# A mixer layer with window attention: projections ahead of their heads, a bounded scale for v, swapped keys by transfer

## The chip, the cores and the metric

The kernel runs on one core of a Trainium2 chip. The metric is the device time of one execution in microseconds. The kernel before took 1007.05 us in the median of three runs (1006.83 to 1008.2).

## What is computed

One layer of a diffusion backbone on 1024 latent tokens (a grid of 16 rows by 64 columns) and 128 context tokens, D = 1024, in float32:

```
h = rmsnorm(x, norm_g) * (1 + scale) + shift            # shift, scale, gate: silu(cond) @ w_ada + b_ada
q, k, v, z_a, u_b, z_b, u_c, z_c, g_a, g_b, g_c = split(h @ w_in)
q, k = rmsnorm(q, q_g), rmsnorm(k, k_g)                 # 8 heads of 64
y_a = softmax over an 8 x 16 window + 128 cached keys   # context tokens: plain attention
y_b = real(fft2(u_b)) @ w_fnet ;  y_c = (window means - u_c) @ w_pool * pool_scale
merged = sum over a, b, c of sigmoid(g) * ((silu(z) * y) @ p)
out = x + gate * (merged @ w_o)                         # also returned: the context tokens' k and v
```

## The kernel before

The tokens are 9 tiles of 128 (tile 8 is the context). Large products are made of three matmuls each (mm3, L143 to L146): both operands are split into a high and a low half of 16 bits (or of rounded float32), and high x high, high x low and low x high are added in PSUM. A weight tile is prepared by a generator (prep, L101): load of the raw weights (L108), sums of squares on ScalarE (L74), a scale that is a power of two (L83 to L91, with a matmul on PE and a power on GpSimd), then the split on ScalarE and VectorE (L98, L99). Raw tiles share NR = 8 slots.

The stages, in order of time: (1) the start, to 69.6 us. The adaLN weights (wa, 16 transfers of 512 KB) and x (9 of 512 KB) are loaded; PE makes the adaLN products (L347) and transposes x (L334) into xT; scale_h (L365) finds a scale for h from a bound. make_h (L385) writes per block k of 128 channels hh and hl, the two halves of h: two ScalarE instructions, two multiply-adds and a subtraction of VectorE (L388 to L391). (2) The early tiles: five token tiles of head pair 0's projection are accumulated beside make_h. (3) The attention stage. A projection of a pair is p1_tiles (L269): per token tile 24 matmuls for q, k and v of two heads, then p1_evac (L214: squares, their sums, a power on GpSimd in rs, v to vraw and its largest value per token) and, half a tile later, p1_norm (L231: four VectorE products into tk, then the halves of q and k into tok, k's high half twice). open_pair (L733) sets a pair up at its first item: pair_setup loads cached keys and values and the bias tables gt; setup_group transposes q and k into q, ka and kb (kb holds the halves of k in swapped order, so that two matmuls give all the products); setup_v finds the largest value of v through PE (pm, pu) and writes v16, and 16 transfers write the windows vw. A pair has 18 items (16 windows of 128 queries, 2 of context), and each goes through five steps one item apart: stage_a scores and bias, stage_b exponential, stage_c transposes, stage_d the product with v, stage_e the transposition of the result py. Between them fill(n) puts n steps (3 matmuls each) of the next pair's projection, 4 an item; beside the last pair those of the u tiles, 6 an item. (4) z and u tiles of branches c and b, the pooling and the Fourier products; (5) P products; (6) za and its P product; (7) the merge gates; (8) the output projection. m_ahead (L191) prepares the weight tile of the next 128 columns in the stages with z and u: load before chunk 0, squares after it, scale after chunk 1, split after chunk 2.

Program order is not the order on the chip. A planner with its own cost model orders the instructions of each engine; it follows the program but moves an instruction ahead when its engine would idle and its operands and buffers are free in the model. It also makes the semaphores. On the chip each engine runs its list in order, and all DMAs stand in one such list, SP's queue. PSUM has eight banks: p1 2, s 2, pt 2, po 1, tr 1.

## Time and profile before

| | |
|---|---|
| median of 3 runs | 1007.05 us |
| the profiled execution, its span | 1008.8 us, 1007.0 us |
| TensorE (PE) busy | 927.9 us (92%) |
| VectorE (DVE), ScalarE (ACT), GpSimd (POOL) busy | 671.1, 523.5, 196.5 us |
| mean granted TensorE clock | 0.977 |

The span is what lies between the first and the last instruction. A busy time is the union of an engine's instructions; matmuls are pipelined, so that two which start 0.16 us apart are shown as 0.33 us long each, and the ends are modelled. A wait is idle time of an engine just before an instruction, with what released it.

### The profile page before, as it was taken

Reading aid. Unit: us, or ns where it says so; the run is one execution under the profiler, and the core shown is the slowest. Engines: PE = TensorE matmul, PEld = TensorE weight load, DVE = VectorE, ACT = ScalarE, POOL = GpSimd, SP = SyncE. Lnnn points to the kernel's source line nnn. Section 1 sums busy time; section 2 is a strip of 40 time slices with the busy share of each in tenths; the row PEclk is TensorE's granted clock in tenths of the full one; section 3 lists DMA queues with packets and bytes.
Section 4 is the critical chain, followed back from the end, with each engine's and each line's share of the span. In section 5 each row is a group of like instructions: output and inputs, shape, how many; then the busy total and the mean of one; then the engine's idle time right before and its main releaser. Section 6 shows DMA issues by size and latency. Waiting matters only on the chain. (4 is left out here: it accounts for less than half of the span.)

```text
span 1007.0 us, 17776 instructions
## 1 busy us (share of the span) xinstructions
PE 927.9 (92%) x6591; PEld 680.3 (68%) x6591; DVE 671.1 (67%) x1568; ACT 523.5 (52%) x1127; POOL 196.5 (20%) x337
## 2 busy tenths in 40 slices
PE   5879897897899899979999899999999999989998
PEld 1325465565666666637897479888888888867886
DVE  1168687677777645696564459878888788766422
ACT  3586766766866856444444534545455444433100
POOL 0114344344344211121200320003021020200000
PEclk9879999999999999979999999999999999999999
DMA  7752223122213322411488502453434332249421
GB/s 274 274 175 80 73 55 72 36 62 66 50 53 63 84 80 82 147 37 53 150 295 301 199 19 95 140 179 98 140 125 152 117 113 92 62 139 307 131 94 53
DMA packets 67415, 121.35 MB, mean 121 GB/s; under 512 B 10064, under 2 KB 34556, under 8 KB 67329
## 3 DMA queue, kind: packets, MB, share of 16 engines
q1 hardware_dynamic: 67329, 120.22, 37.2%
q8 instruction: 52, 0.85, 0.3%
q14 instruction: 34, 0.28, 0.1%
HBM read 87.15 MB, written 28.84 MB: 115 GB/s over the span
## 5 line engine op out<-in xcount | busy, mean ns | idle before, releaser
L144 PE MATMUL p<-wh_q,hh 128*128 128x384 f16 x288 | 96.5, 335 | 1.9 <-ACT hh L388 1.9
L145 PE MATMUL p<-wl_q,hh 128*128 128x384 f16 x288 | 96.2, 334 | 0.0
L146 PE MATMUL p<-wh_q,hl 128*128 128x384 f16 x288 | 94.2, 330 | 0.0
L144 PE MATMUL wo<-woh,mh 128*128 128x512 f32 x144 | 57.1, 396 | 3.6 <-ACT mh L1340 3.6
L146 PE MATMUL wo<-woh,ml 128*128 128x512 f32 x144 | 56.6, 394 | 0.0
L145 PE MATMUL wo<-wol,mh 128*128 128x512 f32 x144 | 56.4, 394 | 0.0
L622 ACT ACTIVATE sn<-sn,mn 128x512 f32<-128x512 f32 x64 | 46.3, 724 | 16.7 <-DVE mn L611 15.7
L635 DVE TENSOR_TENSOR pts<-pt,pts 128x512 f16<-128x512 f32 (+1 forms) x72 | 46.0, 639 | 10.9 <-ACT pts L634 10.9
L611 DVE CUSTOM_DVE_ANT_0 sn<-s,bias 128x512 f32<-128x512 f32 x64 | 43.8, 684 | 12.5 <-PE s L607 12.1
L235 DVE SCALAR_TENSOR_TENSOR tk<-p,rs,grow 128x64 f32<-128x64 f32 x144 | 31.8, 276 | 25.6 <-POOL rs L222 25.6
L1381 DVE TENSOR_TENSOR yo<-wo,gb 128x512 f32<-128x512 f32 x18 | 12.4, 691 | 52.4 <-PE wo L146 52.3
L144 PEld LDWEIGHTS <-wh_m 128*128 128x128 f16 x288 | 29.1, 101 | 24.4 <-ACT wh_m L98 5.8
L145 PEld LDWEIGHTS <-wh_m 128*128 128x128 f16 x288 | 28.8, 100 | 23.5 <-issue 7.5
L88 POOL TENSOR_SCALAR wsc_g<-wsc_g 128x1 f32<-128x1 f32 x12 | 2.8, 231 | 209.0 <-DVE wsc_g L87 209.0
L651 PEld LDWEIGHTS <-pts 128*128 128x128 f16 x792 | 34.9, 99 | 12.2 <-DVE pts L635 6.5
L146 PEld LDWEIGHTS <-wl_m 128*128 128x128 f16 x288 | 28.5, 99 | 20.9 <-issue 1.7
L144 PEld LDWEIGHTS <-hh 128*128 128x128 f16 x288 | 29.0, 101 | 19.4 <-ACT hh L388 2.0
L146 PEld LDWEIGHTS <-hl 128*128 128x128 f16 x288 | 28.7, 100 | 18.7 <-issue 1.4
L634 ACT CAST pts<-pt 128x512 f16<-128x512 f32 (+1 forms) x72 | 38.9, 541 | 3.5 <-PE po L651 1.6
L632 PE MATMUL pt<-ident,sn 128*128 128x128 f32 x256 | 40.0, 277 | 0.8 <-ACT q L506 0.7
L651 PE MATMUL po<-vw,pts 128*128 128x64 f16 x576 | 33.9, 195 | 7.4 <-DVE pts L635 4.3
L145 PEld LDWEIGHTS <-hh 128*128 128x128 f16 x288 | 28.8, 100 | 17.4 <-issue 1.5
(650 smaller groups left out, 3087.6 us busy)
## 6 DMA issues: line engine op xcount, KB each, us to landing
wa<-in_wss_dram SPq DMA_DIRECT2D x16, 512.0 KB
wr_q<-in_w_dram SPq DMA_DIRECT2D x16, 384.0 KB
wr_m<-in_w_dram SPq DMA_DIRECT2D x24, 256.0 KB
pp_c<-pec SPq DMA_DIRECT2D x24, 192.0 KB
pp_b<-peb SPq DMA_DIRECT2D x24, 192.0 KB
pp_a<-pea SPq DMA_DIRECT2D x24, 192.0 KB
ppxc<-pp_c SPq DMA_DIRECT2D x16, 288.0 KB
ppxb<-pp_b SPq DMA_DIRECT2D x16, 288.0 KB
```

The costliest lines, as they stand in the source:

```text
L88: G.tensor_scalar(sc_[:, 2:3], sc_[:, 2:3], 1e-36, None, op0=ALU.max)
L144: T.matmul(out, lh, rh, start=first, stop=False)
L145: T.matmul(out, lh, rl, start=False, stop=False)
L146: T.matmul(out, ll, rh, start=False, stop=last)
L235: ins = V.scalar_tensor_tensor(tkv[:, g], pt[:, g * 64:g * 64 + 64], rs[:, g:g + 1], toks["g"][:, g], op0=ALU.mult, op1=ALU.mult)
L611: V.tensor_tensor_reduce(out=sn, in0=pS, in1=bt.rearrange("p a b -> p (a b)"), op0=ALU.add, op1=ALU.min, scale=1.0, scalar=3e38, accum_out=mn)
L622: S.activation(e[:, :n], it["sn"], AF.Exp, bias=it["mn"], scale=-1.0, accum_out=sm_)
L632: T.transpose(pt[:, j * P:(j + 1) * P], it["e"][:, j * P:(j + 1) * P], ident)
L634: S.copy(pts[:, 0, :n], pt[:, :n])
L635: V.tensor_tensor(pts[:, 1, :n], pt[:, :n], pts[:, 0, :n], op=ALU.subtract)
L651: T.matmul(po[:, :64], it["pts"][:, a, j * P:(j + 1) * P], it["vl"][j][:, c_ * 64:(c_ + 1) * 64], start=(j == 0 and i == 0), stop=(j == nk ...
L1381: V.tensor_tensor(yo, pt, gb[0 if t == 8 else 1][:, cols], op=ALU.mult)
```

## The change

The projection of a pair becomes part of one generator (chain) that also issues the set-up of the pairs at given steps; it starts 41 steps ahead of the first item, gains on the items until item 15, and then keeps its distance. The tiles that two pairs now use at a time have twice the buffers. v is scaled by a bound (from the bound of h, the weights' scale and the largest cached value), so that p1_evac writes its halves straight from PSUM. kb is written by transfers that swap the halves of ka. h is kept in float32 in xT before its scale is known, and make_h then takes one instruction on each of two engines. x and wa are loaded in another order and with more buffers. Weights of z and u are loaded two tiles ahead, and their squares, scale and split come one chunk earlier. The tr bank becomes a second po bank. Cut to its core:

```diff
-NR = 8
-NWA = 4
+NR = 6
+NWA = 6
...
-    BANKS = {"p1": 2, "s": 2, "pt": 2, "po": 1, "tr": 1}
+    BANKS = {"p1": 2, "s": 2, "pt": 2, "po": 2}
...
+        def m_load(i):
+            if i < len(MORDER):
+                munits[i] = prep_m(MORDER[i], f"m{i}")
+                run(munits[i], 1)
         def m_ahead(i, c):
-            if i + 1 < len(MORDER) and i + 1 not in munits:
-                munits[i + 1] = prep_m(MORDER[i + 1], f"m{i + 1}")
-            if i + 1 < len(MORDER):
-                n = {-1: 1, 0: 1, 1: 1, 2: 9}[c]
-                r = run(munits[i + 1], n)
-                if c == 2:
+            if c == -1 and i + 2 < 9:
+                m_load(i + 2)
+            if c == -1 and i == 8:
+                m_load(10)
+            if c == -1 and i > 8:
+                m_load(i + 2)
+            if i + 1 < len(MORDER) and c < 2 and not (c == -1 and i == 8):
+                g = munits[i + 1]
+                n = {-1: 1, 0: 1, 1: 9}[c] + (i == 8 and c == 0)
+                r = run(g, n)
...
+            def new_pair(p, wu):
+                inv = wu["inv"]
...
+                f = qkv.tile([P, 4], F32, tag="vf", name=f"vf{p}", bufs=3)
+                i8, sv, un, scv = (f[:, i:i + 1] for i in range(4))
+                G.tensor_scalar(i8, inv, 0.125, None, op0=ALU.mult)
+                V.tensor_tensor(sv, vrec[:, p:p + 1], inv, op=ALU.mult)
+                V.tensor_tensor(sv, sv, svb, op=ALU.min)
+                pow2(sv)
+                V.reciprocal(un, sv)
+                V.tensor_tensor(un, un, inv, op=ALU.mult)
+                V.reciprocal(scv, un)
+                v16 = qkv.tile([P, 9, 2, 2, 64], F16, tag="v16", name=f"v16{p}", bufs=2)
...
+                rg = qkv.tile([P, 4, 64], F32, tag="rg", name=f"rg{p}_{t}", bufs=2)
+                G.tensor_tensor(rg, c["g"], rs.unsqueeze(2).to_broadcast([P, 4, 64]), op=ALU.mult)
+                pv = pt[:, 256:384].rearrange("p (h d) -> p h d", h=2)
+                S.activation(c["v"][:, t, :, 0, :], pv, AF.Copy, scale=c["sv"])
+                V.scalar_tensor_tensor(c["v"][:, t, :, 1, :], pv, c["sv"], c["v"][:, t, :, 0, :], op0=ALU.mult, op1=ALU.subtract)
...
-                for g in range(4):
-                    ins = V.scalar_tensor_tensor(tkv[:, g], pt[:, g * 64:g * 64 + 64], rs[:, g:g + 1], toks["g"][:, g],
-                                                 op0=ALU.mult, op1=ALU.mult)
-                    tc.keep_in_program_order(ins)
+                V.tensor_tensor(tk, pt[:, :256], rg.rearrange("p g d -> p (g d)"), op=ALU.mult)
...
-                S.copy(qv[:, :, 0], tkv[:, 0:2])
-                S.copy(kv[:, :, 0], tkv[:, 2:4])
-                V.tensor_tensor(qv[:, :, 1], tkv[:, 0:2], qv[:, :, 0], op=ALU.subtract)
-                V.tensor_tensor(kv[:, :, 1], tkv[:, 2:4], kv[:, :, 0], op=ALU.subtract)
-                S.copy(kv[:, :, 2], kv[:, :, 0])
-                toks[t] = t16
...
+                t16 = qkv.tile([P, 4, 2, 64], F16, tag="tok", name=f"tok{p}_{t}", bufs=9)
+                S.copy(t16[:, :, 0], tkv)
+                V.tensor_tensor(t16[:, :, 1], tkv, t16[:, :, 0], op=ALU.subtract)
+                c["toks"][t] = t16
...
+                XG = ((0, 1, 2), (3, 4, 5), (6, 7, 8))
...
+                    V.reciprocal(shs, hm[:, 0:1])
+                    pow2(shs)
...
+                def h_full(k, eng):
+                    for a, c in ((slice(0, NS), 1), (slice(NS, NT), 0)):
+                        if eng is S:
+                            S.activation(xT[:, k, a], xT[:, k, a], AF.Identity, bias=sh[:, k, c:c + 1], scale=gs[:, k, c:c + 1])
+                        else:
+                            V.tensor_scalar(xT[:, k, a], xT[:, k, a], gs[:, k, c:c + 1], sh[:, k, c:c + 1], op0=ALU.mult, op1=ALU.add)
                 def make_h(k):
-                    h32 = st.tile([P, NT], F32, tag="xt", name=f"h32_{k}", bufs=5)
-                    for a, c in ((slice(0, NS), 1), (slice(NS, NT), 0)):
-                        S.activation(hk(hh, k, a), xT[:, k, a], AF.Identity, bias=sh[:, k, c:c + 1], scale=gs[:, k, c:c + 1])
-                        V.tensor_scalar(h32[:, a], xT[:, k, a], gs[:, k, c:c + 1], sh[:, k, c:c + 1], op0=ALU.mult, op1=ALU.add)
                     a = slice(0, NT)
-                    V.tensor_tensor(hk(hl, k, a), h32, hk(hh, k, a), op=ALU.subtract)
+                    S.activation(hk(hh, k, a), xT[:, k], AF.Copy, scale=shs)
+                    V.scalar_tensor_tensor(hk(hl, k, a), xT[:, k], shs, hk(hh, k, a), op0=ALU.mult, op1=ALU.subtract)
...
+                for what in (0, 1, 2, "w0", "w1", 3, 4, 5, "w2", "w3", "w4", "w5"):
+                    load_x(what) if isinstance(what, int) else load_wa(int(what[1:]))
+                nwa = 6
...
+                    if i == 1:
+                        xnorms(XG[0])
+                        run(xg, 8)
+                        for t in XG[2]:
+                            load_x(t)
+                    while nwa < 16 and nwa - 6 <= i:
+                        load_wa(nwa)
+                        nwa += 1
...
+                    if i == 9:
                         run(prep0, 1)
                     if i % 4 == 3:
                         ada_end(i // 4)
+                    if i == 11:
+                        for k in range(6):
+                            h_full(k, (S, V)[k % 2])
                     if i == 13:
+                        run(prep0, 1)
...
+                    if k == 1:
+                        h_full(6, V)
+                    if k == 2:
+                        h_full(7, S)
...
+                    if k == 3:
+                        v_bound(hm)
+                        head_scales(kall)
+                        v_scales(vall)
+                        c0 = new_pair(0, wu)
...
+                def load_bias(c, hd):
+                    p = c["p"]
+                    g = at.tile([P, 1008], F32, tag="gt", name=f"gt{p}_{hd}", bufs=3)
+                    src = bass.AP(tensor=rpbp.tensor, offset=(2 * p + hd) * 23 * 63,
+                                  ap=[[63, 8], [1, 16], [1, 993]])
+                    nc.sync.dma_start(g[:, :993], src)
+                    c["gt"][hd] = g
...
+                def pair_loads(c):
+                    p = c["p"]
                     kr = at.tile([P, 2, P], F32, tag="kr", name=f"kr{p}", bufs=1)
                     nc.sync.dma_start(kr, kctx[p])
                     vr = at.tile([P, 3, 2, 64], F32, tag="vr", name=f"vr{p}", bufs=1)
                     nc.sync.dma_start(vr, vctx[p].rearrange("p (r h d) -> p r h d", r=3, h=2))
-                    gt = []
+                    ka = at.tile([P, 2, 1280], F16, tag="ka", name=f"ka{p}", bufs=2)
+                    kb = at.tile([P, 2, 1280], F16, tag="kb", name=f"kb{p}", bufs=2)
+                    c.update(kr=kr, vr=vr, ka=ka, kb=kb, q=[], bias={}, yt={}, vw=[], gt={})
+                    load_bias(c, 0)
...
+                def swapped(dst, src):
+                    nc.sync.dma_start(dst[0:64], src[64:P])
+                    nc.sync.dma_start(dst[64:P], src[0:64])
...
+                    S.copy(part(c["ka"]), pk if g == 0 else pk.rearrange("p h (a c) -> p h a c", a=2))
+                    for o in ((0,), (512, 1024))[g]:
+                        b = slice(o, o + (512, 256)[g])
+                        swapped(c["kb"][:, :, b], c["ka"][:, :, b])
...
-                    m1 = at.tile([P, 2], F32, tag="m1", name=f"m1{p}", bufs=1)
-                    V.tensor_reduce(m1, vt["mx"].rearrange("p t h -> p h t"), axis=AX.X, op=ALU.max)
-                    pm = bank("tr", f"pm{p}")
-                    T.transpose(pm[:2, :P], m1, ident)
-                    m2 = at.tile([2, 1], F32, tag="m2", name=f"m2{p}", bufs=1)
-                    V.tensor_reduce(m2, pm[:2, :P], axis=AX.X, op=ALU.max)
-                    V.tensor_scalar(m2, m2, 1e-30, 1.0 / 8192, op0=ALU.max, op1=ALU.mult)
-                    dg = at.tile([2, 2], F32, tag="dg", name=f"dg{p}", bufs=1)
-                    V.tensor_scalar(dg, ident[:2, :2], m2, None, op0=ALU.mult)
-                    pu = bank("tr", f"pu{p}")
-                    T.matmul(pu[:, :2], ones8[:2], dg, start=True, stop=True)
...
+                    zb = at.tile([P, 2, P], F16, tag="pqb", name=f"pqb{p}", bufs=2)
+                    swapped(zb, z[:, 2:4])
...
+                def chain():
+                    for p in range(5):
...
+                        elif p < 4:
+                            wu = nextw["wu"]
+                            c = pairs[p] = new_pair(p, wu)
+                            at_(10, pair_loads, c)
+                            at_(14, setup_prompt, c)
+                            at_(18, next_load)
+                            at_(24, pair_cached, c)
+                            for n in (36, 42, 48, 53, 58, 63):
+                                at_(n, next_step)
+                            at_(46, group_q, c, 0)
+                            at_(50, group_k, c, 0)
+                            if p == 3:
+                                at_(66, m_load, 1)
+                            gen = p1_tiles(c, (8, 0, 1, 2, 3, 4, 5, 6, 7), wu)
...
+                        if p > 0:
+                            b = pairs[p - 1]
+                            at_(2, windows, b)
+                            at_(5, group_q, b, 1)
+                            at_(7, group_k, b, 1)
+                        for n, _ in enumerate(gen):
+                            for f, a in ev.get(n, ()):
+                                f(*a)
+                            yield
...
+                fill(32 + 9)
+                LEAD = 16
+                done, want = 9.0, 9.0
                 for j in range(-2, len(items) + 2):
-                    q = 6 if j >= 3 * NI - 2 else 4
-                    if j + 2 < len(items):
-                        it = items[j + 2]
-                        if (j + 2) % NI == 0:
-                            open_pair(it["p"])
-                        if (j + 2) % NI == 1 and it["p"] > 0:
-                            setup_group(cur["c"], it["p"], 1)
-                        if (j + 2) % NI == 12 and it["p"] < 3:
-                            cur["npq"] = setup_prompt(cur["ntk"], it["p"] + 1)
-                        it["c"] = cur["c"]
+                    it = j + 2
+                    want += (72 - 9) / (LEAD - 1) if it < LEAD - 1 else (312 - 72) / (len(items) + 4 - LEAD + 1)
+                    q = int(want - done + 1e-6)
+                    done += q
...
+                    if m == 7:
+                        m_load(9)
...
```

## Rows read from the trace of the kernel before

**Rows 1.** The page: its first line, PE's busy time, and GB/s in 40 slices of 25.2 us
```profile
span 1007.0 us, 17776 instructions
...
PE 927.9 (92%) x6591; PEld 680.3 (68%) x6591; DVE 671.1 (67%) x1568; ACT 523.5 (52%) x1127; POOL 196.5 (20%) x337
...
GB/s 274 274 175 80 73 55 72 36 62 66 50 53 63 84 80 82 147 37 53 150 295 301 199 19 95 140 179 98 140 125 152 117 113 92 62 139 307 131 94 53
```

**Rows 2.** Stretches: length, busy us per engine (instructions), granted PE clock, DMA share, GB/s
```profile
240.00:260.00 20.00, 14.83 (x135) 10.63 (x135) 14.55 (x44) 12.60 (x38) 7.30 (x14) 0.91 0.21 54
...
420.00:440.00 20.00, 14.19 (x78) 8.64 (x76) 19.36 (x31) 8.85 (x17) 6.54 (x5) 0.89 0.11 33
440.00:460.00 20.00, 18.00 (x100) 11.60 (x99) 16.89 (x38) 9.82 (x22) 5.03 (x7) 0.86 0.22 67
460.00:1007.00 547.00, 530.91 (x3531) 432.62 (x3528) 369.95 (x653) 227.20 (x410) 56.65 (x67) 0.99 0.42 140
```

**Rows 3.** PE's waits over the span: waiting line, releaser, us in total, times, longest
```profile
PE py L662 <- DVE yt L653: 10.6, 3, 5.4
...
PE zb L144 <- ACT wh_m L98: 5.4, 1, 5.4
...
PE po L651 <- DVE pts L635: 4.3, 6, 1.0
PE pk L512 <- DVE pts L635: 3.7, 3, 1.2
...
PE pu L545 <- DVE dg L543: 2.8, 3, 0.9
PE po L651 <- DVE yt L653: 2.8, 3, 1.2
PE pq L504 <- DVE tok L248: 2.7, 3, 2.0
...
PE pqp L527 <- DVE tok L248: 2.4, 1, 2.4
```

**Rows 4.** ACT's timeline, 236 to 246 us: start, duration, instruction, idle before, releaser
```profile
241.51 0.63 ACT L74 ACTIVATE wjk_m<-wr_m 128x512 bf16<-128x512 f32 x1 [5.12 <-DMA wr_m<-in_w_dram]
```

**Rows 5.** PE's timeline, 59 to 93 us: start, duration, instruction, idle before
```profile
59.17 1.88 PE L347 MATMUL pa<-wa,sil 128*2 128x512 f32 x4
...
69.60 0.50 PE L144 MATMUL p<-wh_q,hh 128*128 128x384 f16 x1 [1.94 <-ACT hh L388]
...
92.54 0.33 PE L144 MATMUL p<-wh_q,hh 128*128 128x384 f16 x1
92.70 0.33 PE L145 MATMUL p<-wl_q,hh 128*128 128x384 f16 x1
...
93.02 0.22 PE L504 MATMUL pq<-id,tok 128*128 128x128 f16 x1
```

**Rows 6.** Stretches of the start, columns as in rows 2
```profile
8.00:20.00 12.00, 9.28 (x16) 1.50 (x16) 1.53 (x6) 5.69 (x11) 1.29 (x2) 1.00 1.02 406
24.00:30.00 6.00, 6.00 (x29) 2.55 (x27) 0.00 (x0) 2.64 (x5) 0.00 (x0) 1.00 0.48 146
```

**Rows 7.** Waits of SP's DMA queue over the span, columns as in rows 3
```profile
SPq L478 <- POOL bias L585: 74.6, 5, 23.3
...
SPq L294 <- PE pa L347: 18.6, 9, 4.4
```

**Rows 8.** Groups by form, 69 to 430 us: count, busy us, mean ns, idle before
```profile
L235 DVE SCALAR_TENSOR_TENSOR tk<-p,rs,grow 128x64 f32<-128x64 f32 x144 | 31.8, 276 | 25.6 <-POOL rs L222 25.6
...
L584 POOL TENSOR_TENSOR bias<-mk,gt 128x256 f32<-128x256 bf16 x24 | 17.0, 710 | 0.1
...
L391 DVE TENSOR_TENSOR hl<-h,hh 128x1152 f16<-128x1152 f32 x8 | 11.1, 1402 | 0.1
...
L512 PE MATMUL pk<-id,tok 128*128 128x128 f16 x128 | 10.2, 220 | 4.9 <-DVE pts L635 3.7 <-DVE tk L235 0.8 <-DVE tok L249 0.3
```

**Rows 9.** POOL's timeline, 156 to 157 us, columns as in rows 4
```profile
156.04 1.22 POOL L584 TENSOR_TENSOR bias<-mk,gt 128x256 f32<-128x256 bf16 x1
```

More of the change, by code (lines that the diff above doesn't have):

```diff
@@ L713, in start_gen @@
[L713 to L724 removed]
+                pairs = [c0, None, None, None]
```

391 lines of the change are left out of this document (174 added, 217 removed).

## The prediction

> **What bounds the kernel now.** I read the page first [rows 1]: TensorE (PE) is busy for 927.9 of 1007.0 us, more than any other engine, so time can be won where PE waits or works slowly, and by taking PE work away. Next the table of stretches [rows 2]: from 460 us to the end PE is busy for 530.9 of 547 us at a granted clock of 0.99. That stretch holds the pool and Fourier branches' end, the P products, the merge gates and the output projection, and almost nothing is left there to win. Before 460 us it is otherwise: 14.8 of 20 us busy at a pair boundary (240 to 260), 14.2 of 20 where the zc and zb tiles meet (420 to 440). The list of PE's waits [rows 3] names the losers: the transpose py behind yt (10.6 us in 3 waits), zb behind its weights (5.4 us in one), and six smaller ones, of which pk, pu, pq and pqp are the set-up of a head pair. What is behind py is seen on ScalarE (ACT) [rows 4]: it stood 5.12 us at 241.51 on the squares of a weight tile (wjk_m) whose transfer had not landed; these squares are needed only much later, but everything of the attention that ACT has to do stood behind them, and so did VectorE (DVE) and PE. The granted clock of that stretch is 0.91 [rows 2]: PE came back from the wait at the lower of its two levels (1.2 instead of 2.4 GHz). Last, the start: the first projection matmul (p) runs at 69.60 us [rows 5], and until then PE only has the adaLN products and the transposes of x.
>
> **The change part by part.** The sum is made against the profiled execution: 1008.8 us, of which 1007.0 is the span; the median of the runs shown is 1007.05, 1.75 lower.
>
> *The start (loads of x and wa).* Six wa and six xt buffers instead of four and five; x comes in groups of three; the 1.57 MB of the first pair's weights are issued behind all of wa. What must land before the scale of h is known is 9 x and 16 wa transfers of 512 KB, 13.1 MB. The first slice of the page (25.2 us at 274 GB/s) brought 6.9 MB of that [rows 1]. With the engines full the rate is 406 GB/s; from 24 to 30 us it was 146 [rows 6], because the queue stood: it waited 18.6 us in 9 pieces for PE to free wa buffers [rows 7]. If the new order keeps the engines full, the remaining 6.3 MB (with the small tables) take 15.5 us, and the last wa is there at 40.7. From the last adaLN product to the first p matmul it took 69.60 - 59.17 = 10.4 us [rows 5]; the new chain to the scale has as many steps (one more maximum, no multiplication of gs and sh). So the first p matmul comes at 51.1 at the earliest. The weights land 3.9 us behind wa and need some 5 us, which is no later. The buffers still make the queue wait for PE now and then, so I add 4 us and take 55: **-14.5 us**. The bounds are 51.1 (-18.5) and, if the queue stands as before and the weights come behind it, 73.5 (+3.9).
> The Trainium skill (DMA: Bandwidth & Descriptors, Specifications) gives a limit of about 358 GB/s per core from HBM. The 406 GB/s of the row is over it, so the measurement decides; by the page the 6.3 MB would take 17.6 us and the start would be 2.1 us later.
>
> *The early tiles (h in float32, then scaled).* Per block of h, DVE did two forms of multiply-add and a subtraction; now one instruction of 128x1152 (the subtraction took 1.40 us [rows 8]) does it once the scale is known, and the multiply-adds come before it for six blocks. Into this stretch move head_scales, v_scales, v_bound and new_pair, some 30 short DVE instructions with round trips to PE. Before, the stretch from the first p to the first pq took 93.02 - 69.60 = 23.4 us [rows 5], and 120 matmuls at the step of 0.16 us (92.54 to 92.70 [rows 5]) are 19.5. DVE will have about 8 x 1.40 for h, 4 splits and the short ones: as long as PE. I take **+2 us** (0 to +4).
>
> *The attention stage.* The projection of a pair now ends some three items before its heads begin, and its set-up (group_q, group_k, prompt, windows) is spread over the filler steps. What goes: setup_v with its round trip to PE (pu, 2.8), the waits of pq (2.7) and pqp (2.4) for a fresh tok, and pk behind pts (3.7), since half of the pk transposes go and the rest use the po banks: 11.6 us [rows 3]. Their cover is the lead: three items have at least 3 x 12 filler matmuls of 0.16 us, 5.9 us, where a wait for tok was 2.4 at most. What is late next is py: the squares of later weights may still be put ahead of the attention's work on ACT, with six raw buffers instead of eight, but the transfers are written further ahead of them and the bias tables, for which the queue stood 74.6 us [rows 7], get a third buffer. I take half of py's 10.6, 5.3, and one of the two clock losses behind them (0.09 x 20 us, 1.8 [rows 2]). The two po waits (4.3 and 2.8) get a second bank for po, shared with pk, py and the scales: 2. The 64 pk transposes that go are 10.2 us / 2 = 5.1 at most [rows 8]. Together **-25.8 us**; the bounds are -5.1 (every wait comes back under another name) and -38 (all the rows named here, both clock losses).
> Off PE's path, so at nothing: four tk instructions per tile become one, 31.8 us of DVE [rows 8] for 36 x 0.47 (between 0.276 for 64 columns and 1.40 for 1152); maxima of v become a subtraction; three copies on ACT become one; POOL gets one product of 128x256 per tile, 36 x 0.71 = 25.6 us [rows 8], between rs and tk. Its cover is the second p1 bank: a tile needs 24 x 0.16 = 3.9 us of PE even without attention beside it. Without that cover 0.71 us per tile, 26 us, would show.
> The swapped keys are 8 transfers a pair on SP's queue, of 64 partitions each. The trace has none like it; they are between nothing and the 5.12 us that ACT waited for a transfer behind a busy queue [rows 4]. Group 1's are asked for three items before the first item that reads them, 5.9 us of filler alone, so I take nothing; uncovered, 8 groups of them cost 41 us.
>
> *The weights two tiles ahead.* Squares, scale and split of the next weights each come one chunk of 24 matmuls earlier, 3.9 us. zb waited 5.4 [rows 3], so 1.5 remain. The clock of the two stretches around it was 0.89 and 0.86 [rows 2], 0.25 x 20 = 5.0 us; with so short a wait I take 4.0 of it back: **-7.9 us** (0 to -10.4). DVE is full there (19.4 of 20 us [rows 2]), which is the doubt. The rest of the kernel: 0.
>
> The sum: 1008.8 - 14.5 + 2 - 25.8 - 7.9 = 962.6; less 1.75 for the median, **961 us**.
>
> **The rivals.**
> 1. *The waits in the attention stage change their names.* PE's filler and attention come from in-order queues, and DVE stays at three quarters [rows 2]; if a tk behind the longer POOL chain holds up sn or pts, only the removed transposes count. Against it: the waits named stand at set-ups that no longer exist. 961 + 20.7 = 982.
> The Trainium skill (SBUF — State Buffer, Who interferes with whom) says that a DVE instruction with two SBUF inputs and a GpSimd instruction that reads SBUF exclude each other. The trace agrees where it can be seen: at 156.04 POOL's product took 1.22 us [rows 9], its mean is 0.71 [rows 8]; the new product on POOL is of the same form, and stands where such subtractions of DVE are common.
> 2. *The start does not move*, because the transposes of x and the adaLN products free the buffers no sooner than now [rows 7]: 961 + 14.5 = 975.5.
> 3. *All of it goes*: -18.5, 0, -38 and -10.4 give 942.
> 4. *The squares stand more often behind a late transfer: slower.* SP's queue is one queue in order. It now also carries 32 swap transfers, each waiting for an ACT copy, and the raw weight tiles have six slots, so a load stands behind a split of the tile before. Each time ACT meets such squares too soon, PE loses 5.1 us [rows 4] and 1.8 of clock, 6.9 together. It happened three times, twice for long [rows 3]. The change's 46 us are gone from 7 more such stalls; by the code 40 raw tiles are loaded, so there is room for 9: 961 + 62 = 1023. Against it: a load now comes a whole tile ahead of its squares, and the longest waits of the queue, those for the bias tables, have an extra buffer.
> That the change does not do what it says could be so in one respect: the order of instructions is made by a planner that already moves loads and squares far ahead, so "ahead" in the code may be no more than it did before. That is inside rivals 1 and 2.
>
> **How the numbers follow.** Forecast (950 to 969) 0.45; rival 1 and its halves (970 to 990) 0.20; rival 2 0.13; rival 3 0.13; rival 4 0.06; something between, no difference, 0.03. The range 940 to 990 takes in the bounds of the start and of the attention stage and leaves out rival 4 and the far ends. What a measurement of this kernel can tell from no change is 0.2%, 2 us: faster 0.91, within it 0.03, slower 0.06.
>
> **What would show it.** Start: first p matmul near 55 us, DMA near 406 GB/s without the gap at 24 to 30. Attention: pu gone, pq, pk and pqp gone from PE's waits, py at half. Middle: zb's wait under 2 us and a granted clock of 1.00 around it. From there to the end no difference. The forecast is wrong if the first p matmul comes after 65 us, if s waits for the swapped half of the keys, or if ACT's waits for wr transfers become longer or more than in the trace of before.

## The result

The changed kernel takes 996.95 us (median of four runs, 995.81 to 999.48), the kernel before, run beside it, 1007.62 us: a ratio of 0.988 [0.983, 0.993]. It is faster, but by some 11 us and not by the 46 of the forecast, and 997 lies outside the range. The profiled execution is the slowest of the four, 999.48 us; PE is busy for 11.7 us less than in [rows 1], at a granted clock of 0.979:

```profile
span 997.7 us, 17549 instructions
...
PE 916.2 (92%) x6510; PEld 675.4 (68%) x6510; DVE 648.5 (65%) x1431; ACT 495.0 (50%) x1023; POOL 228.5 (23%) x373
```

The landmarks on PE's timeline, of the kernel after (columns as in [rows 5]), cut it into the stages of the sum:

```profile
62.94 0.84 PE L144 MATMUL p<-wh_q,hh 128*128 128x384 f16 x2
...
88.85 0.22 PE L572 MATMUL pq<-id,tok 128*128 128x128 f16 x1
...
94.92 0.29 PE L572 MATMUL pq<-id,tok 128*128 128x128 f16 x1 [5.85 <-DVE tok L279]
...
130.13 0.31 PE L649 MATMUL s<-pqz 128*128 128x128 f16 x1
...
397.58 0.33 PE L144 MATMUL zc<-hh,wh_m 128*128 128x384 f16 x1
...
472.65 0.39 PE L144 MATMUL ppc<-th,oh_pc 128*128 128x384 f32 x1
...
533.02 0.33 PE L144 MATMUL za<-hh,wh_m 128*128 128x384 f16 x1
```

Before, the first p and pq stood at 69.60 and 93.02 [rows 5], and zc, ppc and za at these times:

```profile
401.74 0.33 PE L144 MATMUL zc<-hh,wh_m 128*128 128x384 f16 x1
...
485.30 0.39 PE L144 MATMUL ppc<-th,oh_pc 128*128 128x384 f32 x1
...
542.57 0.33 PE L144 MATMUL za<-hh,wh_m 128*128 128x384 f16 x1
```

| stage, us | before | after | moved | forecast |
|---|---|---|---|---|
| start, to the first p | 69.60 | 62.94 | -6.7 | -14.5 |
| early tiles, to the first pq | 23.4 | 25.9 | +2.5 | +2 |
| attention, to the first zc | 308.7 | 308.7 | 0.0 | -25.8 |
| middle, to the first ppc | 83.6 | 75.1 | -8.5 | -7.9 |
| P products, to the first za | 57.3 | 60.4 | +3.1 | 0 |
| the rest | 464.4 | 464.7 | +0.3 | 0 |

Of the miss of 36.9 us (999.5 for 962.6), 25.8 lie in the attention stage, which gave nothing; 7.8 lie in the start and 3.1 in the P products. PE's waits over the span show what is gone and what came (those of before are [rows 3]):

```profile
PE pq L572 <- DVE tok L279: 19.5, 8, 5.9
...
PE po L702 <- DVE pts L686: 7.5, 10, 1.9
...
PE zb L146 <- DVE wl_m L99: 1.9, 2, 1.4
...
PE py L713 <- DVE yt L704: 1.2, 2, 0.7
```

py fell from 10.6 to 1.2 us, more than half; pu is gone, pk behind pts too (1.8 us stand there behind another releaser), and pqp went from 2.4 to 2.0. But pq, which was to go, rose from 2.7 to 19.5 us, and po behind pts from 4.3 to 7.5. Ahead of both stands a VectorE instruction, tk: tok is made from it, and pts comes later in VectorE's list. Here are VectorE's wait at it over the span of the kernel after, and the groups by form from 60 to 420 us (the tk row of before is in [rows 8], with 25.6 us of waiting):

```profile
DVE tk L271 <- POOL rg L257: 52.6, 34, 3.5
```
```profile
L271 DVE TENSOR_TENSOR tk<-p,rg 128x256 f32<-128x256 f32 x36 | 15.3, 424 | 52.6 <-POOL rg L257 52.6
...
L257 POOL TENSOR_TENSOR rg<-grow,rs 128x256 f32<-128x256 f32 x36 | 22.1, 614 | 2.8
```

tk's own work fell from 31.8 to 15.3 us, near the 16.9 reckoned; its wait doubled.

Two parts of the attention stage moved in opposite directions. The *opening*, from the first pq to the first score matmul s, grew from 21.5 to 41.3 us. About 4 us of this is work that the lead moved into it (108 p matmuls for 84, at a step of 0.16 us). For the rest PE loses both time and clock: it is idle for 16.0 us instead of 4.4, at a granted clock of 0.80 instead of 1.00. The *body*, from the first po to the end of the last py, shrank from 280.2 to 258.9, by 15.2 us of PE's busy time and 6.1 of its idle time. The stretches of the opening, first before, then after, columns as in [rows 2]:

```profile
93.02:114.55 21.53, 17.17 (x123) 9.74 (x121) 15.97 (x55) 16.70 (x42) 12.73 (x21) 1.00 0.27 85
```
```profile
88.85:130.13 41.28, 25.31 (x148) 15.04 (x146) 21.30 (x65) 19.61 (x41) 21.48 (x36) 0.80 0.34 89
```

### The profile page after: what moved, and what is told of

Same layout as the page of the kernel before. It is cut to its first block, busy times and chain, and to the rows that moved or that the text cites. A ratio compares the mean times of both kernels' runs of the same rounds, so it can differ in the third digit from the quotient of the medians.

```text
span 997.7 us, 17549 instructions
## 1 busy us (share of the span) xinstructions
PE 916.2 (92%) x6510; PEld 675.4 (68%) x6510; DVE 648.5 (65%) x1431; ACT 495.0 (50%) x1023; POOL 228.5 (23%) x373
## 4 chain that ended last, share of the span: by engine, by line
PE 65%; DVE 11%; DMA 8%; POOL 7%; ACT 5%; issue 3%; SPq 1%; ACTq 0%; DVEq 0%; POOLq 0%
PE wo L144 3%; PE wo L145 3%; PE wo L146 3%; PE xc L146 3%; PE xb L144 3%; PE xb L146 3%; PE xb L145 3%; PE xc L144 3%; PE xc L145 3%; POOL rs L255 3%; PE xa L144 3%; PE xa L146 3%; PE xa L145 3%; PE ppa L144 2%; PE ppa L146 2%
## 5 line engine op out<-in xcount | busy, mean ns | idle before, releaser
L271 DVE TENSOR_TENSOR tk<-p,rg 128x256 f32<-128x256 f32 x36 | 15.3, 424 | 52.6 <-POOL rg L257 52.6
L145 PEld LDWEIGHTS <-hh 128*128 128x128 f16 x288 | 29.0, 101 | 17.8 <-issue 1.9
L362 PE MATMUL pa<-wa,sil 128*2 128x512 f32 x64 | 31.0, 633 | 10.1 <-DMA wa<-in_wss_dram 10.1
```

Of the source, the lines that this page charges most:

```text
L145: T.matmul(out, lh, rl, start=False, stop=False)
L271: V.tensor_tensor(tk, pt[:, :256], rg.rearrange("p g d -> p (g d)"), op=ALU.mult)
L362: T.matmul(pa[:2], sil[:, k], wa[i][:, q], start=(k == 0), stop=(k == KT - 1))
```

## The experiments

All are edits of the kernel after; ratios are to the kernel before, run beside them. The theory at first was that the opening waits for its set-up; the rivals were the new GpSimd product rg with VectorE's place for tk, and the queues of DMAs.

**The start.** One kernel issues the first wa transfer ahead of x and holds the squares of x behind the condition's exponential; another leaves out half of PE's adaLN products.

```diff
-S.activation(sq, xt[t], AF.Square, scale=1.0 / 32, ...)
+S.activation(sq, xt[t], AF.Square, scale=c32, ...)
...
+c32 = st.tile([P, 1], F32, name="c32")
+V.tensor_scalar(c32, ex[:, 0:1], 0.0, 1.0 / 32, op0=ALU.mult, op1=ALU.add)
...
-for what in (0, 1, 2, "w0", "w1", 3, 4, 5, "w2", ...):
+for what in ("w0", 0, 1, 2, "w1", "w2", 3, 4, 5, ...):
```


> The changed kernel with the first adaLN weight tile loaded ahead of x, and the exponential of the condition tied ahead of ScalarE's squares of x; nothing else. Theory A (PE bounds the start): from the first adaLN product (12.89 us) to the last (54.1) PE has 41.7 us of work and stands for 1.6, so the start moves by as much as the first product moves: it comes at about 9.3, the first projection matmul at 59 to 60 in place of 62.9, and the time is 993 to 995 us. Rival B (the transfers bound it, as the prediction had it): the bytes are the same, so the first projection matmul stays within 1 us of 62.9 and the time within 1 us of 997.


```diff
-for q in range(2):
+for q in range(1):
...
```


> The changed kernel with every second adaLN product left out (32 of 64 matmuls of 2 x 512; all transfers stay), so the shift and scale are of half of the condition. Theory A (PE bounds the start): 15.5 us of PE's 41.7 go; the start shortens until the transfers bound it, so the last adaLN product comes at 40 to 45 us in place of 54.1, the first projection matmul at 49 to 54, and the transfers run near 400 GB/s to the end of wa. Rival B (the transfers bound it already): the last adaLN product comes no earlier than 52 us.

With wa first the first adaLN product ran at 8.54 instead of 12.89 us, but the last ended only 1.5 us sooner and the first p came at 61.43 (from 62.94); s gained 0.5. The whole: 998.66 us, ratio 0.988 [0.985, 0.991], no different from the kernel after. With half the adaLN work (one run, 1000.3 us) the last product still ended at 52.94 (from 54.10), the first p came later, at 65.62, and SP's queue waited longer for PE, 23.2 us; the two rows are of the kernel after and of the one with half the products:

```profile
SPq L308 <- PE pa L362: 17.9, 8, 5.9
```
```profile
SPq L308 <- PE pa L362: 23.2, 8, 9.7
```

So PE's amount of work alone does not set the end. With half of it PE stood 6.3 us at the transposes of x behind VectorE's xt and 3.0 us at pb behind ScalarE's ar, and the granted clock in the three stretches of 10 us from 20 to 50 us was 0.77, 0.89 and 0.83, where the kernel after had 1.00. In PE's list adaLN products stand behind transposes of x, those behind the norms, and those behind x; that this order is the cause was not tested by itself.

**The opening, by its waits.** Four kernels change the place of the set-up: group_q, group_k and the prompt later in the chain; the scales of the cached keys held behind a tile; the same with the bias tables; the squares of the next weights held behind tile 2.

```diff
-at_(4, group_q, c, 0); at_(6, group_k, c, 0); at_(14, setup_prompt, c)
+at_(20, group_q, c, 0); at_(22, group_k, c, 0); at_(24, setup_prompt, c)
```


> The changed kernel with the transposes of pair 0's q and k (group_q, group_k, setup_prompt) at steps 20, 22 and 24 of its chain in place of 4, 6 and 14; nothing else. Theory A (PE's order): the eight transposes stand in PE's queue ahead of projection matmuls whose operands have long been there, so PE stands 6.0 and 2.3 us behind tok and comes back at the lower clock; then these waits go, the granted clock between 80 and 100 us rises from 0.82 to above 0.95, the first transpose of probabilities comes about 10 us earlier, and the kernel takes 986 to 990 us where the changed one takes 997. Rival B (the chain of each tile): the tokens come no faster than the chain squares, sum, power, product, tk, tok through four engines lets them, some 3 to 4 us a tile, so the wait moves to the last tile's transposes near 120 us and the time stays within 2 us of 997.


```diff
+V.scalar_tensor_tensor(tz[:, 0:2], c["rs4"][:, 0:2], 0.0, ksp, op0=ALU.mult, op1=ALU.add)
...
-f = ks_[:, 2 * p + hd:2 * p + hd + 1]
+f = ksp[:, hd:hd + 1]
```


> The changed kernel with the cached keys and values of pair 0 (kh, vc) tied to the fifth early tile by a product with zero, so that ScalarE can't reach them before the first squares of the projection. Theory A: ScalarE stood 5.15 us on the transfer of kr ahead of the first squares (sq at 82.78 us), and all of the opening stands behind that; then sq comes some 4 us earlier, the first wait of pq falls from 6.0 to about 2 us, and the kernel takes 991 to 994 us. Rival B: the first tile's squares also need PE's last matmul of that tile and the scale from VectorE (79.3 us), and GpSimd's long product stands until 77 us; then it is at most 1.5 us earlier and the time is within 2 us of 997.


```diff
...
+if p == 0:
+    for r_ in ((0,) if rb == 0 else (0, 12)):
+        G.tensor_copy(b[:, r_, 0:4], c["rs4"])
```


> The changed kernel with two kinds of work held back until the fifth early tile of pair 0 has its scale (by a product with zero or a copy that is overwritten): the cached keys and values (kh, vc) on ScalarE, and the bias tiles of pair 0 on GpSimd. Nothing else. Moving the wait of PE (groups_late) brought the first scores only 2 us earlier, holding back kh alone 1.2 us. Theory B (the chain of each tile): GpSimd is the narrow place of it, and stands 1.1 us on the transfer of gt with 5 us of bias work among the powers of the first four tiles; then the tokens of tiles 0 to 3 come at 91 to 92 us in place of 97.2, the first scores at 124 to 126 in place of 130.1, and the kernel takes 991 to 993 us where the changed one takes 997. Rival C (the late tiles): the last tiles 5, 6 and 7 wait for banks and for transfers of weights near 115 to 122 us anyway; then the first scores come no earlier than 128.5 and the time is within 2 us of 997.


```diff
-S.activation(jk[:, :n], r, AF.Square, scale=1.0 / 16384, ...)
+S.activation(jk[:, :n], r, AF.Square, scale=sc16, ...)
...
```


> The changed kernel with the squares of the weights of pairs 2 and 3 and of the first u weights tied to the third tile of the pair before (one copy and one small product a pair), so that ScalarE cannot come to them before their transfers are in. Theory C: ScalarE stands 0.84 and 1.42 us on a transfer of wr_q at 117 and 121 us, with the squares of the last early tile behind it; then that tile's token comes 2 to 4 us earlier than 125.7, the first scores at 126 to 128 in place of 130.1, and the kernel takes 993 to 995 us. Rival B: the tile's token is late by its own chain, the first scores move by less than 1 us and the time by less than 1.5.

None opened it. With the groups later the two pq waits before 98 us (7.9 us) were gone, and 7.1 us stood instead at pk and at p behind tk: s gained 2.0, 995.13 us (0.985 [0.982, 0.988]). The others gained 1.2, 1.0 and 1.5 us at s, and the last two, which tie work of later pairs too, lost about 5 us in the body: 997.81 (0.988 [0.985, 0.991]), 1004.6 (0.995 [0.993, 0.998]) and 1000.79 us (0.991 [0.988, 0.994]). The theory of the set-up fell.

**The chain on GpSimd.** One kernel takes the power and rg of pair 0 off GpSimd (its power is left out); one moves rg of all pairs to VectorE.

```diff
-G.tensor_scalar(rs, ss, EPS, None, op0=ALU.add)
-G.tensor_tensor(rs, rs, mhalf, op=ALU.pow)
+if p == 0: V.tensor_scalar(rs, ss, EPS, None, op0=ALU.add)
+else: ...
-G.tensor_tensor(rg, c["g"], ...)
+(V if p == 0 else G).tensor_tensor(rg, c["g"], ...)
```


> The changed kernel with GpSimd taken out of the normalization of pair 0: the sum with epsilon and the product rg on VectorE, and the power (-0.5) left out, so that q and k of the first two heads are scaled wrongly. Pairs 1 to 3 are as in the changed kernel. Theory B (the chain of each tile through GpSimd sets the pace of the opening): 1.9 us of GpSimd and two rounds between engines go from each of nine tiles; pq's waits near 89 to 97 us fall from 8.3 to under 4 us, the token of the last tile of pair 0 comes at 112 to 116 us in place of 126.2, and the first scores at 117 to 121 in place of 130.1. Rival C (the late tiles wait for their projection, banks and transfers): the first scores come no earlier than 126 us.


```diff
-G.tensor_tensor(rg, c["g"], rs.unsqueeze(2).to_broadcast([P, 4, 64]), op=ALU.mult)
+V.tensor_tensor(rg, c["g"], rs.unsqueeze(2).to_broadcast([P, 4, 64]), op=ALU.mult)
```


> The changed kernel with the product rg (128 x 256, one a tile, 36) on VectorE in place of GpSimd. The prediction costed it at nothing, with the second p1 bank as its cover. Theory B (GpSimd's chain sets the pace of the opening): 0.61 us and a round between two engines go from each of nine tiles; the first scores come 3 to 5 us earlier, pq waits less for tok in each pair, and the kernel takes 992 to 994 us. Rival: the second bank covers it as predicted; the first scores move by less than 1 us, VectorE has 36 x 0.4 us more, and the time is within 1.5 us of 997.

Without the chain the opening is 26.9 us long instead of 41.3, with the same 108 p matmuls: PE is idle in it for 5.5 us instead of 16.0, at a granted clock of 0.96. The first bias sum sn stood at 126.25 instead of 139.24, the time of the one run was 988.53 us. The stretch of the opening without the chain (columns as in [rows 2]), and PE's waits from 60 to 137 us, first of the kernel after, then without the chain:

```profile
89.76:116.66 26.90, 21.44 (x149) 13.27 (x147) 21.63 (x74) 18.69 (x41) 6.51 (x14) 0.96 0.47 125
```
```profile
PE pq L572 <- DVE tok L279: 15.1, 4, 5.9
```
```profile
PE pq L575 <- DVE tok L282: 4.7, 3, 4.3
```

What the chain is for one tile is seen in the timelines of POOL, VectorE and ScalarE of the kernel after; the last step of GpSimd is what VectorE waits for, and ScalarE behind it:

```profile
88.69 0.24 POOL L254 TENSOR_SCALAR rs<-ss 128x4 f32<-128x4 f32 x1
89.39 1.03 POOL L255 TENSOR_TENSOR rs<-rs,mhalf 128x4 f32<-128x4 f32 x1
90.50 0.61 POOL L257 TENSOR_TENSOR rg<-grow,rs 128x256 f32<-128x256 f32 x1
```
```profile
91.14 0.42 DVE L271 TENSOR_TENSOR tk<-p,rg 128x256 f32<-128x256 f32 x1 [3.48 <-POOL rg L257]
```
```profile
91.60 0.41 ACT L278 CAST tok<-tk 128x256 f16<-128x256 f32 x1 [3.11 <-DVE tk L271]
```

On VectorE rg brought s 4.6 us sooner, but the body lost 9.8: 1003.84 us (nine of ten runs, 1000.94 to 1007.19; 0.995 [0.993, 0.997]). VectorE's one queue carries the attention too, which is the likely reason.

**What stands behind the waiting tk.** One kernel calls p1_norm three steps later, and the group set-ups with it; one makes the high halves on GpSimd instead of ScalarE.

```diff
-if k == 3 and late:
+if k == 6 and late:
...
-at_(5, group_q, b, 1); at_(7, group_k, b, 1)
+at_(8, group_q, b, 1); at_(10, group_k, b, 1)
```


> The changed kernel with a tile's normalization (tk, tok) issued at step 6 of the next tile in place of step 3 (and group_q, group_k of the second half at steps 8 and 10 in place of 5 and 7, since they read it). Theory R (the first rival of the prediction): between 137 and 397 us VectorE stands 36.4 us in 25 waits at tk for GpSimd's rg, and ScalarE 31.9 us at tok behind it, with the softmax of the heads queued behind both; asked for three steps (9 matmuls, 1.5 us, and the attention between them) later, these waits fall by a third or more, PE's waits for pts fall from 7.5 to below 5 us, and the kernel takes 991 to 994 us. Rival: the order on the engines is made by the planner, which moves tk and tok ahead again, and a bank is held longer; waits and time stay as they are, within 1.5 us of 997.


```diff
-S.copy(t16[:, :, 0], tkv)
+G.tensor_copy(t16[:, :, 0], tkv)
```


> The changed kernel with the first half of the token (tok, the copy of tk, 36 of 128 x 256) on GpSimd in place of ScalarE. Theory R: ScalarE's in-order queue stands 31.9 us in 26 waits at tok for tk, with exponentials and pts behind it; without it ScalarE is free for pts, PE's waits po behind pts (7.5 us) fall by half and the stretch from the first po to the last py is 3 to 6 us shorter than 258.9. Rival: VectorE waits in ScalarE's place (its second half of tok then waits for GpSimd, 0.6 us later), and the stretch is as long or longer.

Three steps later: 994.68 us (0.985 [0.982, 0.988]), some 3 us by the ratios, whose intervals overlap; s came 4.5 us sooner. On GpSimd: 1011.44 us, no faster than the kernel before (1.002 [1.000, 1.004]), with a body of 271.9 us; ScalarE then waited 55 us at sn behind mn, where it had waited 29.

**The two edits at tk, one by one.** Two things were done to tk at once: one product with rg from GpSimd took the place of four that read rs, and the line that kept the four in program order went. The first kernel puts the order back; the second puts the four products back, without the order; the third both; the fourth keeps the order and adds later norms (with the group set-ups) and slots of their own for the P weights.

```diff
-V.tensor_tensor(tk, pt[:, :256], ...)
+tc.keep_in_program_order(V.tensor_tensor(tk, pt[:, :256], ...))
```


> The changed kernel with tk kept in program order among VectorE's instructions, nothing else; the product rg stays on GpSimd and the issue at step 3. It splits what the old normalization gave (972.95 us in place of 997). Theory R1 (the place in the order): VectorE's waits at tk fall from 36.4 to below 25 us, the stretch from the first po to the last py from 258.9 to 250 or less, and the kernel takes 986 to 992 us. Theory R2 (GpSimd's extra step): program order at step 3 is too early for the chain through rg; the waits stay above 30 us and the time within 3 us of 997. In both the opening stays at 40 us or more from the first pq to the first scores.


```diff
-G.tensor_tensor(rg, c["g"], rs.unsqueeze(2).to_broadcast([P, 4, 64]), op=ALU.mult)
...
-V.tensor_tensor(tk, pt[:, :256], ...)
+for i in range(4):
+    V.scalar_tensor_tensor(tk[:, i * 64:(i + 1) * 64], pt[:, i * 64:(i + 1) * 64], rg[:, i:i + 1], c["g"][:, i],
+                           op0=ALU.mult, op1=ALU.mult)
```
In this kernel and the next, p1_evac returns rs, so that rg in p1_norm is rs.


> The old normalization (four multiply-adds straight from rs, no rg on GpSimd) without the mark that keeps them in program order. Theory R2 (GpSimd's extra step): most of what it gave stays, 973 to 979 us. Theory R1 (the order): the planner moves the four ahead of pts and yt as it did with tk, VectorE waits for rs as the kernel before did or more (20 us and over between the first po and the last py), and the kernel takes 983 to 990 us.


```diff
+    tc.keep_in_program_order(V.scalar_tensor_tensor(...))
```


> The changed kernel with the normalization of the kernel before: four multiply-adds of 128 x 64 on VectorE straight from rs, in program order, in place of rg on GpSimd and one product on VectorE. The prediction took one product in place of four as free. Theory B and R (GpSimd's extra step is on the path): the opening from the first pq to the first scores, 41.3 us, falls to 36 to 38, the stretch from the first po to the last py is no longer than 258.9, and the kernel takes 990 to 994 us. Rival: the four products cost VectorE 36 x 0.7 us more on the same path (the product on VectorE cost the stretch 9.8 us), and the time is 997 to 1005.


```diff
+tc.keep_in_program_order(V.tensor_tensor(tk, ...))
-if k == 3 and late:
+if k == 6 and late:
...
-raw = wp.tile([P, WU], F32, tag="wr", ..., bufs=NR)
+raw = olp.tile([P, 512], F32, tag="or", ..., bufs=4)
...
```


> The changed kernel with tk kept in program order among VectorE's instructions (as the kernel before had it) and issued at step 6 of the next tile in place of step 3 (group_q, group_k of the second half at steps 8 and 10), and with four raw slots of their own for the P products' weights. Theory R: the planner had moved tk ahead of pts and yt, and VectorE stood there 36.4 us in 25 waits for GpSimd's rg; behind them the waits fall below 20 us, the stretch from the first po to the last py falls from 258.9 to 250 to 255 us, and the kernel takes 985 to 990 us. Rival: VectorE's waits are not on PE's path (PE waits for pts only 7.5 us in all), a bank and the next tile's squares come later, and the stretch stays above 257 us; then the time is that of the later issue alone, 992 to 995.

| | median, us | ratio to before | opening | body |
|---|---|---|---|---|
| before | 1007.62 | 1 | 21.5 | 280.2 |
| after: rg, order free | 996.95 | 0.988 [0.983, 0.993] | 41.3 | 258.9 |
| rg, order kept | 983.52 | 0.973 [0.970, 0.976] | 40.9 | 244.2 |
| four products, order free | 990.15 | 0.979 [0.976, 0.982] | 32.4 | 258.1 |
| four products, order kept | 972.95 | 0.964 [0.962, 0.966] | 30.7 | 242.6 |
| rg, order kept, later norms | 980.30 | 0.972 [0.969, 0.974] | 34.9 | 248.7 |

The two effects fall in different places. Read down the columns: rg costs the opening 9 to 10 us and the body next to nothing; the free order costs the body 15 and the opening next to nothing. Together they are 24 us. The fourth kernel changes more than one thing and is no part of this reading. VectorE's wait at tk from 127 to 397 us follows: the kernel after, then order kept, then four products, then both:

```profile
DVE tk L271 <- POOL rg L257: 37.3, 26, 2.4
```
```profile
DVE tk L271 <- POOL rg L257: 17.5, 20, 1.7
...
PE po L702 <- DVE pts L686: 0.9, 2, 0.5
```
```profile
DVE tk L270 <- POOL rs L255: 24.6, 25, 2.0
...
PE po L702 <- DVE pts L686: 6.0, 11, 1.3
```
```profile
DVE tk L270 <- POOL rs L255: 3.7, 10, 0.6
...
PE po L703 <- DVE pts L687: 1.1, 3, 0.5
```

Where the order is free, po waits for pts 6 us and more (7.5 in the kernel after); where it is kept, about 1. VectorE's timelines show the difference: between a tile's sums (L252) and its tk stand 3.2 other instructions in the mean with the order free and 5.4 with it kept (the 27 tiles of pairs 1 to 3), and 2.4 and 5.7 with the four products. With the order free tk stands earlier in VectorE's list; on the chip VectorE stands there, with pts and yt of the attention behind tk. With the order kept PE's idle time in the body falls from 20.2 to 9.1 us, and with the four products from 17.8 to 8.4. The po waits behind pts are 6.6 and 4.9 of this; the rest lies in smaller waits behind VectorE and ScalarE, which were not followed one by one. The line also changes what the planner does with other instructions; how much of the 15 us comes through tk's own place is not shown.

**Weights and raw slots.** One kernel puts the old m_ahead back; two have eight raw slots instead of six, the second with the later groups.

```diff
-if c == -1 and i + 2 < 9:
-    m_load(i + 2)
...
+if i + 1 < len(MORDER) and i + 1 not in munits:
+    m_load(i + 1)
+    return
...
```


> The changed kernel with the preparation of the z and u weights as before: one tile ahead, squares, scale and split one chunk later. Theory: the wait of zb for its weights comes back, 4 to 5 us, with clock behind it, and PE's stalls between the last py and the P products rise from 8.7 to 14 to 16 us; the raw slots are free again, so the stretch of the P products loses the 3 to 4 us that it gained in length. Sum: 1000 to 1003 us. Rival: the u and z tiles had room anyway and only the P products change: 993 to 996.


```diff
-NR = 6
+NR = 8
```


> The changed kernel with eight raw weight slots (NR = 8) in place of six. Theory D: the stretch of the P products of branches c and b lost 3 us against the kernel before since the raw tiles wait for slots that the two weight tiles loaded ahead now hold; with eight, PE's waits for oh_pc, gb and za there (11 us in all) fall by 3 to 5 us, and so does the time, 992 to 994. Rival: these waits are of VectorE's and ScalarE's order; the stretch from 472 to 533 us stays within 1 us of 60.4 and the time within 1.5 us of 997.

> The changed kernel with eight raw weight slots in place of six, and group_q, group_k and setup_prompt of pair 0 at steps 20, 22 and 24 in place of 4, 6 and 14. Alone the slots took 3.4 us off the stretch of the P products (472 to 530 us, 54.1 in place of 57.5), and the later transposes brought the first scores 2 us earlier. If the two add up, the kernel takes 991 to 993 us where the changed one takes 997; rival: the planner makes another order of the opening with more slots (with eight alone the first projection matmul came 3 us later), and it takes 994 to 997.

One tile ahead took 1008.46 us (0.999 [0.998, 1.001]). zb waited 4.7 us for its weights again, and the middle took 80.7 us instead of 75.1, with a granted clock of 0.83 from 420 to 440 us. This row is of that kernel:

```profile
PE zb L144 <- ACT wh_m L98: 4.7, 1, 4.7
```

Its loss by the medians, 11.5 us, is larger than that stage. Its profiled execution is 6.7 us longer than that of the kernel after: 5.6 in the middle, 3.8 in the P products and 1.2 in the attention, with the start and the rest 4 shorter; where the remainder of the medians lies is not known. Eight slots: 996.23 and 998.92 us (0.988 and 0.989), no change; the stretch of the P products was 3.5 us shorter in the first, whose first p came 3.0 us later, and 1.3 longer in the second.

**All that helped.** Four products in order, later norms and wa first:

```diff
+    tc.keep_in_program_order(V.scalar_tensor_tensor(...))
-if k == 3 and late:
+if k == 6 and late:
...
-for what in (0, 1, 2, "w0", ...):
+for what in ("w0", 0, 1, 2, ...):
...
```


> The old normalization in program order, issued at step 6 of the next tile in place of 3 (with group_q, group_k of the second half at 8 and 10), and the first adaLN tile loaded ahead of x. Alone the later issue gave the changed kernel 5 us, the load order 1.5 us at the first projection matmul, which the opening swallowed. With GpSimd's step gone the opening is shorter, and both can show: 966 to 971 us where the old normalization alone takes 973. Rival: VectorE's waits at tk are gone already and banks are held longer: 972 to 977.

972.66 us, 0.961 [0.958, 0.964]: the best of all, but not told apart from the four products in order alone.

## Why the prediction was wrong

**The step that failed** is the work at tk that was "off PE's path, so at nothing": "four tk instructions per tile become one", and "POOL gets one product of 128x256 per tile, 36 x 0.71 = 25.6 us [rows 8], between rs and tk. Its cover is the second p1 bank". The size of the product was nearly right (36 x 0.614 = 22.1 us). Its cover held in the body, where rg costs 0.8 and 1.6 us by the table, though VectorE waits 13 to 14 us longer at tk. It failed in the opening: a second bank lets PE go on with the next tile, but PE soon comes to pq, which needs tok, and tok waits for tk. There rg costs 9 to 10 us, less than the 26 named for the case without cover. Nine tiles of 0.61 us would be at most 5.5 of it, and the granted clock of the opening is 0.80 and 0.81 with rg, 0.88 and 0.92 without; how the rest comes about was not followed. The row to read was there: in [rows 8] tk already waited 25.6 us for rs of GpSimd, so the chain had no time to spare, and only what else PE had to do could cover a longer one.

**A line without a price.** The diff drops the line that kept tk in program order. The forecast did not cost it; it is worth 15 us in the body, more than rg. Both undone, the attention stage is 282.6 us, 26.1 less than before, where the forecast had 25.8: the first pq and the first zc of the kernel with four products in order are

```profile
89.08 0.22 PE L573 MATMUL pq<-id,tok 128*128 128x128 f16 x1
...
371.72 0.33 PE L144 MATMUL zc<-hh,wh_m 128*128 128x384 f16 x1
```

The sum agrees, its terms only in part, so that the agreement is partly luck: in that kernel no wait of py is left, so py fell by 10.6 and not by 5.3, while pq still waits 11.7 us, 6.0 in the opening and 5.8 in the body, where the lead of three items was to cover it. Its opening is 9 us longer than before, some 4 of it moved work; pair 0's set-up has no attention in front of it. The first rival named tk as what holds up pts, at a price of 20.7 us against the 25.8 that were lost. Its reason, the longer chain on GpSimd, is not what the kernels show for pts: with the longer chain and the order kept, po waits 0.9 us for it.

**The start** was sized too well: -6.7 for -14.5. The mechanism was right in part: the gap at 24 to 30 us is gone, and the stretches of the kernel after are (columns as in [rows 6])

```profile
8.00:20.00 12.00, 7.11 (x19) 2.04 (x20) 2.95 (x9) 6.46 (x13) 1.14 (x2) 1.00 1.03 414
24.00:30.00 6.00, 5.21 (x30) 2.73 (x29) 2.64 (x7) 2.60 (x7) 0.87 (x1) 1.00 1.02 407
```

but the queue's waits for PE hardly fell, 18.6 to 17.9 us, and came later instead. The term "I add 4 us" for them should have been about 12: 62.94 less 51.1. The sum went by the transfers; in the kernel after PE itself is busy without a break from 30 to 50 us, while the transfers fall to 246 and 230 GB/s:

```profile
30.00:40.00 10.00, 10.00 (x40) 3.27 (x38) 2.55 (x7) 5.83 (x13) 1.10 (x2) 1.00 0.72 246
40.00:50.00 10.00, 10.00 (x38) 3.18 (x37) 3.68 (x10) 7.29 (x14) 0.00 (x0) 1.00 0.70 230
```

The limit of about 358 GB/s that the Trainium skill gives (DMA: Bandwidth & Descriptors, Specifications) is again below what the trace shows, 414 and 407 GB/s.

**Early tiles** (+2.5 for +2) and **middle** (-8.5 for -7.9) came near what was worked out. zb waits 1.9 us, and the clock around it is 1.00 where [rows 2] had 0.89 and 0.86:

```profile
420.00:440.00 20.00, 17.36 (x100) 10.06 (x99) 19.03 (x35) 9.97 (x19) 7.29 (x8) 1.00 0.07 20
440.00:460.00 20.00, 18.44 (x133) 14.92 (x131) 17.46 (x36) 11.09 (x28) 4.65 (x6) 1.00 0.29 88
```

The old m_ahead gave 5.6 of the 8.5 back, so the cause is shown for that part.

**The P products** took 3.1 us more, which the forecast had at nothing. The slots are not shown to be the cause: with eight, and with slots of their own, the stretch was shorter in one kernel and not in two. Nor is the load two tiles ahead: with the old m_ahead it was 64.2 us. In the kernels whose edits lie elsewhere it is between 59.9 and 64.6 us long, so that 3.1 us is no more than other edits move it by. The cause stays open.

**The other signs**: s does not wait for the swapped half of the keys in the kernel after; of the kernels tried, only the one with the order kept, later norms and slots of their own has such a wait, one of 2.1 us. ScalarE's waits for the transfers of wr became more, as the prediction's sign of being wrong has it, but not longer: 16.9 us in 8 before, 15.9 in 13 after (12.3 of it in 10 at wr_m), the longest 5.1 and 2.5. The fourth rival's long stalls did not come. Its neighbour, the third rival, leaves the 1.75 us of the median out of its sum: its 942 should be 940.

## What to carry to other kernels

Before a step is put into a chain between engines at no cost, look at how long the chain's consumer already waits for it, and ask stage by stage what the busiest engine has to do meanwhile: the same step cost almost nothing beside the attention, and 9 to 10 us in the opening, where PE has no attention beside the projection. A free buffer covers the producer, not what stands behind the consumer in its queue. In an order that a planner makes, a line that ties an instruction to its place is part of a change, and is priced like an instruction. And where a change has many parts, undo the parts at one instruction one by one: here two of them cost 24 us.

## What the runs showed beyond that

The first product of grow on GpSimd, 128x128, took 13.46 us in the kernel after, beside VectorE's writing of hl and wl_q, and 0.40 us in the kernel with half the adaLN products, where it ran behind them:

```profile
63.54 13.46 POOL L232 TENSOR_TENSOR grow<-qgb,gs 128x128 f32<-128x128 f32 x1
```
```profile
78.91 0.40 POOL L232 TENSOR_TENSOR grow<-qgb,gs 128x128 f32<-128x128 f32 x1
```

It ended at 77.0, before rg first needed it at 85.2, so it cost nothing here.
The Trainium skill (SBUF — State Buffer, Who interferes with whom) has the two engines exclude each other in such a case; the trace agrees, and the price, some thirty times the duration, is the trace's.
